# Two mixer attentions put into a written order, slot by slot, with the products of the branches between them

## The chip, the cores and the metric

One core of one Trainium2 chip. TensorE multiplies matrices, VectorE, ScalarE and GpSimd work on tiles, SyncE issues the DMAs; each takes its own instructions in order and waits on semaphores for the others. The metric is the device time of one execution in microseconds (us), as the median of several runs; lower is better.

## What is computed

Two blocks of a network run one after the other on one sequence of 512 positions with 1024 features. The first block has two layers of mixer, cross attention and FFN; only the mixer is touched. Cut to what matters here:

```python
def hybrid_mixer(x, ...):
    aq, ak, av, bq, bk, bv, cz, gate = split(x @ w_in)
    out_a = window_attention(rope(aq), rope(ak), av, sink)          # 8 heads of 64, 2 kv heads, band of 128
    out_b = dense_block_attention(rope(rms(bq)), rope(rms(bk)), bv)  # 8 heads of 64, all 512 keys
    out_c = spatial_gating(gelu(cz))
    gates = sigmoid(gate + b_gate)                                   # 3 branches x 1024
    merged = sum over n of (branch_n @ w_branch[n]) * gates[n]
    return merged @ w_mix_out
```

All products are done in a split form: each operand is rounded to a high part and a remainder, and high x high, high x low and low x high are added.

## The kernel before, in words

**Products.** `mm3` (L128) issues the three matmuls of one product, at L131, L132 and L133. A 128-row weight unit comes through `W` (L135): a 512 KB DMA on SyncE into one of two `wraw` tiles (L141), a rounding copy on ScalarE into one of three `wh` tiles (L146), a subtraction on VectorE into one of three `wl` tiles (L150).

**The mixer** (`mix`, L943) runs `gating` (branch c), then `heads_ab` for a (L726: projections by `tok`, rotary tables by `rope`, then `to_stack`, which transposes the queries on TensorE and splits them into tiles at L621 to L626, and `to_twice`, the same for the keys, L635 to L642), then `attn_a` (L783), `branch` for c (L920), `heads_ab` for b, `attn_b` (L829), `branch` for a and `branch` for b. Branch n makes 8 units: a gate product of 8 x 3 matmuls of 512 columns, a tanh (L930), an output product of 4 x 3 matmuls, and a merge (L938, or L940 and L941).

**One head** of attention: four score tiles (`mm2`, L649 and L650, into one of two `pss` banks), per tile a maximum on VectorE (L805 and L807 in a; L844, and in b L845 for the queries' norm, which is applied at the exponential) and an exponential with a row sum on ScalarE (L809, L847), a reciprocal and four scalings on VectorE (L818, L852), then `pt_av` (L693): transposes on TensorE (L703, two `pt` banks), a rounding copy on ScalarE (L166), a subtraction on VectorE (L167), and two matmuls (L713, L714) into the one `po` bank; `join` (L716) moves and adds the halves (L719, L720).

**What sets the order.** The program is traced in the order above, and the tile framework's planner then orders every engine's instructions when it builds the program (L1832, `schedule_with_timeline_sim=True`): at each moment of its own modelled time it takes, for an engine, the ready instruction that was traced first, and gives tiles their buffers as they come free. Only where a block stands in `behind(mark)` is an instruction held behind the marked one on the same engine. In the attentions and branches of before nothing is held: their interleaving is the planner's.

Of the kernel before, what the change touches and what calls it, by code (L numbers as in the profile page):

```python
# [7 lines left out]
F32R = mybir.dt.float32r  # L8
# [9 lines left out]
NK = 8  # L18
# [31 lines left out]
class Kernel:  # L50
# [76 lines left out]


# [6 lines left out]
    def W(self, ap, kc, tag=None):  # L135

# [8 lines left out]
        for i in range(n):  # L145
            nc.scalar.copy(h[i][:, :e], raw[:, i * e:(i + 1) * e])  # L146
        self.turn += 1
# [9 lines left out]
        return at  # L157
# [535 lines left out]
    def pt_av(self, out, pap, nkt, qr, vap, first=True, last=True, keep=None):  # L693


        nc = self.nc
        for kt in range(nkt):
# [11 lines left out]
            v, o = vap(kt), out[:, q0 * 128:q1 * 128]  # L709
            if isinstance(v, tuple):  # L710
                self.mm3(o, *v, h[:, :n], l[:, :n], first and kt == 0, last and kt == nkt - 1)
                continue
            nc.tensor.matmul(o, v, h[:, :n], start=first and kt == 0, stop=False, skip_group_check=True)  # L713
            nc.tensor.matmul(o, v, l[:, :n], start=False, stop=last and kt == nkt - 1, skip_group_check=True)  # L714

    def join(self, out, o, half):  # L716

        r, q = (slice(64 * i, 64 * i + 64) for i in (half, 1 - half))
        self.nc.scalar.copy(out[r], o[q])  # L719
        self.nc.vector.tensor_add(out[r], out[r], o[r])  # L720
# [5 lines left out]
    def heads_ab(self, l, br, xs, tabs, mid=None):  # L726
# [40 lines left out]
        rs = None  # L767
        if isb:
# [9 lines left out]
            rs = rq  # L778
        Q = [self.to_stack("q", [qt[c // 2, t // 2][:, t % 2, (c % 2) * 128:(c % 2 + 1) * 128] for t in range(4)]) for c in range(4)]
        Kt = self.to_twice("r", [kt[t // 2][:, t % 2, :] for t in range(4)])  # L780
        return Q, Kt, V, rs

    def attn_a(self, qkv, sink):  # L783
        nc = self.nc
        Q, Kt, V, _ = qkv
        nsink = self.sm(8)
        nc.vector.tensor_scalar(nsink, sink, -1.0, None, op0=ALU.mult)
        out = []
        for c in range(4):
            both = self.T("w")  # L790
            for half in range(2):
                o = self.po()
                hd = c + 4 * half
                kh, kl = Kt[half]
                P = []
                mx, nm, sm = self.sm(4), self.sm(4), self.sm(4)
                for qt in range(4):
                    k0, k1 = max(0, qt - 1), min(4, qt + 2)
                    n = (k1 - k0) * 128
                    ps = self.pss()  # L800
                    self.mm2(ps[:, :n], Q[c][half][:, qt * 128:(qt + 1) * 128], kh[:, k0 * 128:k1 * 128],
                             kl[:, k0 * 128:k1 * 128])
                    pt = self.T("vw"[half])
                    m0 = (k0 - qt + 1) * 128
                    nc.vector.tensor_tensor_reduce(pt[:, :n], ps[:, :n], self.mask[:, m0:m0 + n], 1.0, -3e38,  # L805
                                                   op0=ALU.add, op1=ALU.max, accum_out=mx[:, qt:qt + 1])
                    nc.vector.tensor_scalar(nm[:, qt:qt + 1], mx[:, qt:qt + 1], -0.125, nsink[:, hd:hd + 1],  # L807
                                            op0=ALU.mult, op1=ALU.min)
                    nc.scalar.activation(pt[:, :n], pt[:, :n], AF.Exp, bias=nm[:, qt:qt + 1], scale=0.125,  # L809
                                         accum_out=sm[:, qt:qt + 1])  # L810
                    P.append(pt)
                es = self.sm(4)
                nc.scalar.activation(es, nm, AF.Exp, bias=sink[:, hd:hd + 1])
                nc.vector.tensor_add(sm, sm, es)
                nc.vector.reciprocal(sm, sm)
                for qt in range(4):
                    n = (min(4, qt + 2) - max(0, qt - 1)) * 128
                    nc.vector.tensor_scalar(P[qt][:, :n], P[qt][:, :n], sm[:, qt:qt + 1], None, op0=ALU.mult)  # L818

                def pap(qt, kt):  # L820
                    o0 = (kt - max(0, qt - 1)) * 128
                    return P[qt][:, o0:o0 + 128]
                vap = lambda kt: V[kt // 2][:, kt % 2, 128 * half:128 * half + 128]
                self.pt_av(o, pap, 4, lambda kt: (max(0, kt - 1), min(4, kt + 2)), vap)
                self.join(both, o, half)
            out.append(self.split("o", both))
        return out

    def attn_b(self, qkv):  # L829
        nc = self.nc  # L830
        Q, Kt, V, rq = qkv
        out = []
        for c in range(4):
            both = self.T("w")
            for half in range(2):
                o = self.po()
                kh, kl = Kt[half]
                P = []
                nm, sm = self.sm(4), self.sm(4)
                for qt in range(4):  # L840
                    ps = self.pss()
                    self.mm2(ps, Q[c][half][:, qt * 128:(qt + 1) * 128], kh, kl)
                    i = ((c // 2) * 2 + qt // 2) * 8 + (qt % 2) * 4 + (c % 2) * 2 + half
                    nc.vector.tensor_reduce(nm[:, qt:qt + 1], ps, axis=AX.X, op=ALU.max, negate=True)  # L844
                    nc.vector.tensor_tensor(nm[:, qt:qt + 1], nm[:, qt:qt + 1], rq[:, i:i + 1], op=ALU.mult)  # L845
# [992 lines left out]
```

## Time and profile before

| | before |
|---|---|
| median of 3 runs | 3546.34 us (3545.05 to 3547.64) |
| the profiled execution's own time | 3543.88 us |
| its span, first to last instruction | 3542.1 us |
| TensorE busy, matmuls | 3396.8 us (96%), 19136 |
| VectorE, ScalarE, GpSimd busy | 2168.1, 1538.4, 386.6 us |
| mean granted TensorE clock | 0.98 of 2.4 GHz |

Busy matmul time is modelled and overlapping, so a busy share says that TensorE had something, not that it ran at its full pace; the number of matmuls per microsecond and the granted clock say that.

### The profile page before, as it was taken

The numbers are of one execution on the slowest core, as the hardware profiler recorded it, in microseconds if no ns is written. First come the engines' busy times: TensorE is split into PE (matmuls) and PEld (weight loads), VectorE is DVE, ScalarE is ACT, GpSimd is POOL, SyncE is SP. The second block draws the span as 40 slices with busy tenths as digits, with TensorE's granted clock in tenths as the row PEclk, the third lists the DMA queues.
The fourth block names the chain that finished last, engine by engine and source line by source line (L and its number), as shares of the span: only waits on it lengthen the run. The fifth ranks groups of instructions, "written<-read, shape, count | busy, mean of one in ns | idle before, by whom it ended". The sixth has DMA issues, their size and how long they took to land.

```text
span 3542.1 us, 49037 instructions
## 1 busy us (share of the span) xinstructions
PE 3396.8 (96%) x19136; PEld 2953.1 (83%) x19136; DVE 2168.1 (61%) x3926; ACT 1538.4 (43%) x2854; POOL 386.6 (11%) x588
## 2 busy tenths in 40 slices
PE   9989799999999897999999898999999998999999
PEld 8877598888898775998888897889888887988887
DVE  5675577645666755776456688655333698664333
ACT  3454445433444444455334556443222576442222
POOL 0000012000010000020000343000000286110000
PEclk9999899999999997999999998999999999999999
DMA  4312132333323120322333122222333322222333
GB/s 142 89 46 76 30 115 77 90 96 95 107 81 87 46 78 24 112 91 84 100 96 101 58 79 88 82 84 84 95 99 94 100 72 90 78 66 90 101 95 95
DMA packets 87928, 302.38 MB, mean 85 GB/s; under 512 B 10000, under 2 KB 10768, under 8 KB 87696
## 3 DMA queue, kind: packets, MB, share of 16 engines
q1 hardware_dynamic: 87696, 299.24, 28.0%
q8 instruction: 151, 2.47, 0.3%
q14 instruction: 81, 0.66, 0.1%
HBM read 297.10 MB, written 2.10 MB: 84 GB/s over the span
## 4 chain that ended last, share of the span: by engine, by line
PE 83%; DVE 7%; ACT 3%; POOL 3%; issue 2%; DMA 1%; ACTq 0%; POOLq 0%; DVEq 0%
PE mm L131 23%; PE mm L132 23%; PE mm L133 23%; PE pt L703 2%; PE mm L195 1%; PE pss L133 1%; PE pss L132 1%; PE pss L131 1%; DVE wl L150 1%; PE pss L649 1%; PE pss L650 1%; PE mm L198 1%; PE po L195 1%; PE po L714 1%; POOL v L1454 1%
## 5 line engine op out<-in xcount | busy, mean ns | idle before, releaser
L146 ACT CAST wh<-wraw 128x1024 fp32r<-128x1024 f32 (+2 forms) x496 | 514.3, 1040 | 959.8 <-PE mm L132 491.7
L150 DVE TENSOR_TENSOR wl<-wraw,wh 128x1024 fp32r<-128x1024 f32 (+2 forms) x487 | 599.5, 1233 | 501.6 <-ACT wh L146 499.0
L131 PE MATMUL mm<-xh,wh 128*128 128x512 f32 (+1 forms) x2152 | 821.8, 382 | 8.3 <-ACT xh L437 6.0
L132 PE MATMUL mm<-xl,wh 128*128 128x512 f32 (+1 forms) x2152 | 821.5, 382 | 1.2 <-DVE xl L440 1.1
L133 PE MATMUL mm<-xh,wl 128*128 128x512 f32 (+1 forms) x2152 | 819.7, 381 | 0.0
L131 PEld LDWEIGHTS mm<-xh,wh 128*128 128x128 f32 x2152 | 405.9, 189 | 83.6 <-ACT xh L437 6.4
L132 PEld LDWEIGHTS mm<-xl,wh 128*128 128x128 f32 x2152 | 406.1, 189 | 77.4 <-DVE xl L440 3.3
L133 PEld LDWEIGHTS mm<-xh,wl 128*128 128x128 f32 x2152 | 405.9, 189 | 75.8
L131 PE MATMUL mm<-wh,xh 128*128 128x256 f32 x768 | 219.7, 287 | 8.3 <-DVE v L671 8.3
L133 PE MATMUL mm<-wh,xl 128*128 128x256 f32 x768 | 219.6, 286 | 0.0
L132 PE MATMUL mm<-wl,xh 128*128 128x256 f32 x768 | 219.2, 286 | 0.0
L131 PE MATMUL mm<-p,wh 128*128 128x512 f32 (+1 forms) x556 | 202.1, 373 | 12.4 <-ACT p L166 7.7
L133 PE MATMUL mm<-p,wl 128*128 128x512 f32 (+1 forms) x556 | 206.4, 372 | 0.0
L132 PE MATMUL mm<-p,wh 128*128 128x512 f32 (+1 forms) x556 | 205.8, 371 | 0.0
L376 POOL TENSOR_TENSOR s<-s 128x2 f32<-128x2 f32 x14 | 6.8, 483 | 1617.4 <-ACT s L373 1617.4
L131 PE MATMUL mm<-o,wh 128*128 128x512 f32 (+1 forms) x456 | 169.3, 371 | 0.0
L132 PE MATMUL mm<-o,wh 128*128 128x512 f32 (+1 forms) x456 | 169.1, 371 | 0.0
L133 PE MATMUL mm<-o,wl 128*128 128x512 f32 (+1 forms) x456 | 169.1, 371 | 0.0
L1170 DVE TENSOR_TENSOR x<-x,mm 128x512 f32<-128x512 f32 (+1 forms) x102 | 57.0, 566 | 164.4 <-PE mm L133 164.3
L131 PEld LDWEIGHTS mm<-wh,xh 128*128 128x128 f32 x768 | 148.5, 194 | 9.4 <-issue 8.3
L132 PEld LDWEIGHTS mm<-wl,xh 128*128 128x128 f32 x768 | 148.7, 194 | 0.4
L133 PEld LDWEIGHTS mm<-wh,xl 128*128 128x128 f32 x768 | 148.7, 194 | 0.2
(628 smaller groups left out, 7133.3 us busy)
## 6 DMA issues: line engine op xcount, KB each, us to landing
wraw<-fup SPq DMA_DIRECT2D x88, 512.0 KB, 3.6
wraw<-gup SPq DMA_DIRECT2D x88, 512.0 KB, 3.6
wraw<-wg SPq DMA_DIRECT2D x48, 512.0 KB, 3.6
wraw<-wt SPq DMA_DIRECT2D x32, 512.0 KB, 3.6
wraw<-fdn SPq DMA_DIRECT2D x32, 512.0 KB, 3.5
wraw<-gdn SPq DMA_DIRECT2D x32, 512.0 KB, 3.5
wraw<-wbr SPq DMA_DIRECT2D x24, 512.0 KB, 3.6
wraw<-wab SPq DMA_DIRECT2D x20, 512.0 KB, 3.6
```

Source lines behind the costliest of these rows:

```text
L131: mm(out, lh, rh, start=first, stop=False, skip_group_check=True)
L132: mm(out, lh, rl, start=False, stop=False, skip_group_check=True)
L133: mm(out, ll, rh, start=False, stop=last, skip_group_check=True)
L146: nc.scalar.copy(h[i][:, :e], raw[:, i * e:(i + 1) * e])
L150: eng.tensor_tensor(l[i][:, :e], raw[:, i * e:(i + 1) * e], h[i][:, :e], op=ALU.subtract)
L195: self.nc.tensor.matmul(out, w[:, c], xs[k][0][:, t], start=first and k == 0 and w is h, stop=False, skip_group_check=True)
L198: self.nc.tensor.matmul(out, h[:, c], xs[k][1][:, t], start=False, stop=k == kc - 1, skip_group_check=True)
L649: mm(out, q, kh, start=True, stop=False, skip_group_check=True)
L650: mm(out, q, kl, start=False, stop=True, skip_group_check=True)
L703: nc.tensor.transpose(ps[:, i * 128:(i + 1) * 128], pap(qt, kt), self.ident)
L714: nc.tensor.matmul(o, v, l[:, :n], start=False, stop=last and kt == nkt - 1, skip_group_check=True)
L1170: self.nc.vector.tensor_add(x, x, ps)
```

## The change

`attn_a` and `attn_b` become one `attn`, which, like `branch`, no longer issues its work as it goes but lists events (slot, function). `weave` sorts the events of one attention and of the branches given to it by slot, and issues each behind the last one issued on every engine but SyncE, so that inside a weave the order on TensorE, VectorE, ScalarE and GpSimd is that of the slots. A head starts every 12 slots, and so does a branch unit. Attention a is woven with branch c, attention b with branches a and b. `W` is split in three steps (copy, subtraction, use), so that they have slots of their own. The first half of a head's scalings goes from VectorE to GpSimd. In b the norm is multiplied into the queries before the transposes (four 128x512 operations in `heads_ab`), and L845 goes.

```diff
+    def put(self, f):
+        n = len(self.nc.cur_bb.bb.instructions)
+        with self.behind(*self.seq.values()):
+            f()
+        for i in self.nc.cur_bb.bb.instructions[n:]:
+            if i.engine != self.nc.sync.engine:
+                self.seq[i.engine] = i
+
+    def weave(self, events):
+        self.seq = {}
+        for _, f in sorted(events, key=lambda e: e[0]):
+            self.put(f)
...
+            for i, (u, p) in enumerate((u, p) for u in range(2) for p in range(2)):
+                qv = qt[u, p].rearrange("p t (h c) -> p t h c", h=4)
+                r = rq[:, 8 * i:8 * i + 8].rearrange("p (t h) -> p t h", t=2)
+                nc.vector.tensor_tensor(qv, qv, r[:, :, :, None].to_broadcast([128, 2, 4, 64]), op=ALU.mult)
...
+            def norm(a):
+                e = slice(2 * a, 2 * a + 2)
+                if isa:
+                    nc.vector.tensor_add(st["sm"][:, e], st["sm"][:, e], st["es"][:, e])
+                nc.vector.reciprocal(st["sm"][:, e], st["sm"][:, e])
+                eng = nc.vector if a else nc.gpsimd
+                for qt in (2 * a, 2 * a + 1):
+                    p = P[qt][:, :width(qt)]
+                    eng.tensor_scalar(p, p, st["sm"][:, qt:qt + 1], None, op0=ALU.mult)
...
+            for j in range(4):
+                at(s0 + 3 * j, lambda j=j: score(j))
+                at(s0 + 3 * j + 1, lambda j=j: top(j))
+                at(s0 + 3 * j + 2, lambda j=j: exp(j))
+                at(s0 + 3 * j + 15, lambda j=j: turn(j))
+                at(s0 + 3 * j + 16, lambda j=j: high(j))
+                at(s0 + 3 * j + 17, lambda j=j: low(j))
+                at(s0 + 3 * j + 19, lambda j=j: weigh(j))
+            for a in range(2):
+                if isa:
+                    at(s0 + 6 * a + 5.5, lambda a=a: sinks(a))
+                at(s0 + 6 * a + 6, lambda a=a: norm(a))
+            at(s0 + 29, move)
+            at(s0 + 30, join)
+            if half:
+                at(s0 + 31, split_h)
+                at(s0 + 32, split_l)
+        for i in range(8):
+            head(i)
+        for slot, f in fill:
+            at(slot + 0.6, f)
+        self.weave(ev)
...
-    def branch(self, l, n, o, xs, mrg):
+    def branch(self, l, n, o, xs, mrg, s=0, lag=0, add_to=True):
...
+        for gate_ in (0, 1):
+            unit_at(gate_, 0, s - 2, s - 1)
         for k in range(NK):
+            so, sg = (s + 12 * k, s + 12 * k + 4) if k >= lag else (s + 8 * lag + 4 * k, s + 8 * k)
+            if k + 1 < NK:
+                unit_at(1, k + 1, *((so + 1, so + 3) if k >= lag else (sg + 1, sg + 3)))
+                if k % 2 and k >= lag:
+                    unit_at(0, k // 2 + 1, so + 6, so + 9)
...
+            for q in range(4):
+                at(so + q, lambda k=k, q=q: out(k, q))
             for q in range(NK):
+                at(sg + q, lambda k=k, q=q: gate(k, q))
+            at(sg + 8, lambda k=k: tanh(k))
+            e = max(so + 4, sg + 8)
+            at(e + 1, lambda k=k: merge(k))
+            if add_to:
+                at(e + 2, lambda k=k: add(k))
...
-        self.branch(l, 2, oc, xs, mrg)
+        self.attn("a", qkv, sink, oa, self.branch(l, 2, oc, xs, mrg, add_to=False))
...
-        ob = self.attn_b(qkv)
-        self.branch(l, 0, oa, xs, mrg)
-        self.branch(l, 1, ob, xs, mrg)
+        self.attn("b", qkv, None, ob, self.branch(l, 0, oa, xs, mrg) + self.branch(l, 1, ob, xs, mrg, 96, 3))
```

`head(i)` sets `s0 = 12 * i`. `score` is the two matmuls of a tile, `top` the maximum, `exp` the exponential, `turn` the transposes, `high` and `low` the copy and the subtraction after them, `weigh` the two matmuls into `po`, `move` and `join` the former `join`; in `branch`, `out` and `gate` are one `mm3` each, and `unit_at` sets the copy (with the DMA) and the subtraction of a weight unit. The numbers of matmuls, transposes and weight loads are those of before.

## Rows read from the trace of the kernel before

**Rows 1.** The chain that ended last, by engine, share of the span

```profile
PE 83%; DVE 7%; ACT 3%; POOL 3%; issue 2%; DMA 1%; ACTq 0%; POOLq 0%; DVEq 0%
```

**Rows 2.** Windows, first mixer: stretch, busy us and (instructions) per engine, clock, DMA, GB/s

```profile
96.00:190.00 94.00, 94.00 (x518) 81.95 (x517) 56.61 (x127) 46.04 (x89) 0.00 (x0) 1.00 0.27 81
190.00:246.00 56.00, 46.41 (x292) 40.03 (x291) 44.97 (x143) 27.41 (x71) 0.00 (x0) 0.91 0.13 38
246.00:330.00 84.00, 84.00 (x400) 69.91 (x398) 56.44 (x105) 39.53 (x65) 0.00 (x0) 1.00 0.27 83
330.00:423.00 93.00, 71.09 (x281) 47.19 (x279) 55.69 (x116) 44.10 (x87) 0.00 (x0) 0.89 0.06 17
```

**Rows 3.** Windows of the FFN and of `tok`, and transposes in the timeline

```profile
2500.00:2550.00 50.00, 50.00 (x222) 41.40 (x221) 19.20 (x22) 11.77 (x13) 0.00 (x0) 1.00 0.32 95
...
80.00:90.00 10.00, 10.00 (x85) 10.00 (x85) 8.97 (x15) 2.71 (x4) 0.00 (x0) 1.00 0.38 116
...
194.20 0.38 PE L703 MATMUL pt<-ident,w 128*128 128x128 f32 x2
...
194.54 0.49 PE L703 MATMUL pt<-ident,w 128*128 128x128 f32 x3
```

**Rows 4.** Matmuls by tile: ns min/median/max, first and last start us; both mixers

```profile
L131 PE MATMUL mm<-wh,xh x87: 283/283/333, 59.8 to 96.1; 128*128 128x256 f32 x87
...
L649 PE MATMUL pss<-r,q x6: 277/306/339, 121.0 to 133.1; 128*128 128x256 f32 x3, 128*128 128x384 f32 x3
...
L131 PE MATMUL mm<-wh,xh x48: 277/283/415, 220.3 to 245.5; 128*128 128x256 f32 x48
...
L649 PE MATMUL pss<-r,q x6: 389/389/389, 272.9 to 290.8; 128*128 128x512 f32 x6
...
L131 PE MATMUL mm<-p,wh x20: 389/389/389, 428.6 to 463.2; 128*128 128x512 f32 x20
...
L131 PE MATMUL mm<-wh,xh x123: 283/283/333, 1019.9 to 1070.5; 128*128 128x256 f32 x123
...
L131 PE MATMUL mm<-p,wh x20: 389/389/389, 1407.4 to 1442.1; 128*128 128x512 f32 x20
```

**Rows 5.** Groups by form, 96 to 464 us: busy us, mean ns, idle before

```profile
L150 DVE TENSOR_TENSOR wl<-wraw,wh 128x1024 fp32r<-128x1024 f32 x42 | 51.4, 1223 | 44.6 <-ACT wh L146 44.1
L167 DVE TENSOR_TENSOR t<-pt,t 128x512 fp32r<-128x512 f32 x32 | 21.7, 688 | 21.4 <-ACT t L166 21.3
L844 DVE TENSOR_REDUCE s<-pss 128x1 f32<-128x512 f32 x32 | 21.6, 688 | 9.2 <-PE pss L650 9.1
L941 DVE TENSOR_TENSOR m<-m,f 128x512 f32<-128x512 f32 x15 | 10.3, 689 | 0.3
L852 DVE TENSOR_SCALAR w<-w,s 128x512 f32<-128x512 f32 x16 | 6.7, 482 | 0.1
...
L146 ACT CAST wh<-wraw 128x1024 fp32r<-128x1024 f32 x42 | 44.2, 1052 | 60.7 <-PE mm L132 45.7 <-PE mm L133 7.7 <-issue 7.4
...
L847 ACT ACTIVATE w<-pss,s 128x512 f32<-128x512 f32 x16 | 12.3, 774 | 7.6 <-DVE s L845 7.5
L625 ACT CAST q<-pt 64x512 fp32r<-64x512 f32 x16 | 9.3, 582 | 10.5 <-DVE q L626 5.7 <-PE pt L621 4.7
```

**Rows 6.** Timeline of VectorE at the end of `heads_ab` for b

```profile
256.15 0.20 DVE L301 SCALAR_TENSOR_TENSOR s<-s 128x40 f32<-128x40 f32 x1
...
256.86 0.20 DVE L301 SCALAR_TENSOR_TENSOR s<-s 128x40 f32<-128x40 f32 x1
257.10 0.76 DVE L775 TENSOR_TENSOR w<-w,s 128x256 f32<-128x256 f32 x2
```

**Rows 7.** GpSimd: a group by form, then GpSimd and VectorE in the timeline

```profile
L991 POOL TENSOR_TENSOR p<-w,p 128x512 fp32r<-128x512 f32 x4 | 5.6, 1414 | 0.0
...
511.24 0.74 POOL L413 TENSOR_TENSOR x<-x,c 128x256 f32<-128x256 f32 x1 [4.70 <-DVE x L408]
...
511.34 1.72 DVE L150 TENSOR_TENSOR wl<-wraw,wh 128x1024 fp32r<-128x1024 f32 x1
```

More of the change, by code (lines that the diff above doesn't have):

```diff
@@ L135, in W, with W_steps @@
     def W(self, ap, kc, tag=None):
+        steps = self.W_steps(ap, kc, tag)
+        next(steps)
+        next(steps)
+        return next(steps)
+    def W_steps(self, ap, kc, tag=None):
         nc = self.nc
@@ L146, in W @@
             nc.scalar.copy(h[i][:, :e], raw[:, i * e:(i + 1) * e])
+        yield
         self.turn += 1
@@ L156, in at @@
             return h[k // kp][:, s], l[k // kp][:, s]
-        return at
+        yield
+        yield at
     def split(self, role, src, n=512, scale=None):
@@ L708, in pt_av @@
                 h, l = keep[kt]
[L709 to L720, printed above, removed]
+            vh, vl = vap(kt)
+            self.mm3(out[:, q0 * 128:q1 * 128], vh, vl, h[:, :n], l[:, :n], first and kt == 0, last and kt == nkt - 1)
     def wt(self, l, g):
@@ L780, in heads_ab, with attn @@
         Kt = self.to_twice("r", [kt[t // 2][:, t % 2, :] for t in range(4)])
-        return Q, Kt, V, rs
-    def attn_a(self, qkv, sink):
+        return Q, Kt, V
+    def attn(self, br, qkv, sink, out, fill):
         nc = self.nc
[L785 to L845, printed above, removed]
-                    pt = self.T("vw"[half])
-                    nc.scalar.activation(pt, ps, AF.Exp, bias=nm[:, qt:qt + 1], scale=rq[:, i:i + 1],
-                                         accum_out=sm[:, qt:qt + 1])
-                    P.append(pt)
-                nc.vector.reciprocal(sm, sm)
-                for qt in range(4):
-                    nc.vector.tensor_scalar(P[qt], P[qt], sm[:, qt:qt + 1], None, op0=ALU.mult)
-                vap = lambda kt: V[kt // 2][:, kt % 2, 128 * half:128 * half + 128]
-                self.pt_av(o, lambda qt, kt: P[qt][:, kt * 128:(kt + 1) * 128], 4, lambda kt: (0, 4), vap)
-                self.join(both, o, half)
-            out.append(self.split("p", both))
-        return out
@@ L859, in gating @@
+        both = []
+        for i in range(8):
[3 more added lines that the diff above has]
+        self.weave(ev)
     def gating(self, l, xs, cb, bs, oc):
@@ L955, in mix @@
         qkv = self.heads_ab(l, "a", xs, ta, lambda: next(g))
-        oa = self.attn_a(qkv, sink)
-        mrg = {}
-        self.branch(l, 2, oc, xs, mrg)
+        oa, ob, mrg = [], [], {}
+        self.attn("a", qkv, sink, oa, self.branch(l, 2, oc, xs, mrg, add_to=False))
         tb, tq = self.T("c"), [self.T("c"), self.T("c")]
```

129 lines of the change are left out of this document (109 added, 20 removed).

## The prediction, made before the run

> **What bounds the kernel now.** I read the chain of waits first: 83% of it is TensorE [rows 1], so a change pays only where TensorE has something to win back. Then the windows, to find where that is. In the FFN TensorE issues 222 matmuls of 512 columns in 50 us, 0.225 us each; the projections by `tok` (256 columns) take 10 us for 85, 0.118 each; a transpose adds 0.11 (0.38 for two, 0.49 for three) [rows 3]. I call that the dense pace; for 384 columns I take 0.172, halfway.
>
> In the mixer two stretches are dense and two are not [rows 2]. From 96 to 190 us and from 246 to 330 TensorE is busy throughout at clock 1.00: there the planner has woven heads with branch c, and later with branch a. From 190 to 246 and from 330 to 423 it is busy 46.4 of 56 us and 71.1 of 93, at clocks 0.91 and 0.89: the branch that could fill has been used up, or (branch b) needs attention b's output, and the remaining heads run almost alone. VectorE is at 60 to 80% and ScalarE at 47 to 49% in all four, so neither is the bound; it is latency, head after head.
>
> The loss in numbers. The stretch runs from the last `tok` of a's heads (its last high product starts at 96.1) to the last output product of branch b (463.2, with its triple 463.9) [rows 4]: 367.5 us. Its TensorE work at the dense pace:
> - 24 branch units x 36 x 0.225 = 194.4;
> - 8 heads of b: 8 score matmuls 1.8, 8 in `po` 1.8, 16 transposes 1.76; 5.4 each, 42.9;
> - 8 heads of a: 2 x (4 x 0.118 + 4 x 0.172) + 10 x 0.11 = 3.4 each, 27.4;
> - `tok` for b, 288 x 0.118 = 34.0; 40 transposes of queries and keys, 4.4.
>
> Together 303; lost 64. The second mixer runs from 1070.5 to 1442.1 and its triple, 372.3 [rows 4], with the same work: lost 69. **133 us in all is what the change can reach.**
>
> **The change, part by part.**
>
> *The weave itself.* TensorE's work is the same. A period of 12 slots holds one head's attention work and one branch unit: 8.1 + 3.4 = 11.5 us in a, 8.1 + 5.4 = 13.5 in b. VectorE per period in b: 4 maxima and 4 `low` at 0.69, `join`, merge and add at 0.69, half a split 0.34, two scalings 0.96, one and a half weight subtractions 1.83, reciprocals 0.4 by the small operations of [rows 6]: 11.1 us of 13.5 [rows 5]. In a, with tiles 320 columns wide on average and no add, about 9.5 of 11.5. ScalarE: 4 x 0.77, 4 copies and a move at 0.58, a tanh 0.77, half a split 0.3, 1.05 + 0.53 of weight copies: 8.7 [rows 5]. So TensorE is the longest in each period. Does strict order stall it? I placed b's period by hand: the tightest place is the single `po` bank. `weigh` 3 of a head starts 5.0 us into a period; `move` and `join` follow; the next head's first `weigh` is due at 8.35; with VectorE's queue in order, `join` ends near 7.5. Slack 0.9 us. Every other wait (two `pss`, two `pt`, three `mm` banks, three `wh`) has over 1.5 us. So the stall per head lies between 0 (the dense windows of rows 2) and a slipped slot, about 1.1 us; I take 0.5 for 16 heads, **8 us a mixer**.
>
> *Weight loads.* 24 gate and output units as before. The DMAs stay outside the chain, so SyncE issues them when a `wraw` tile is free; a unit comes 12 slots after the one whose tile it takes. Price 0; the cover is those 11 us, and without it a load shows whole.
>
> *The norm put ahead in b.* Off: 32 small operations of about 0.2 us on VectorE. On: four of 512 columns, 0.69 each by L941 [rows 5]. The former were covered; the latter stand before the first score (next).
>
> *The new wait: the start of each weave.* TensorE's chain starts with `score` 0, which needs queries and keys, and every branch product is queued behind it. In before, the gates ran meanwhile: between the last `tok` product and the first score lie 24.9 us in a and 27.4 in b [rows 4], all dense. Now nothing covers this.
> - a: four query stacks, whose copies and subtractions take turns on one bank (copies wait for the subtraction, 5.7 us in all [rows 5]): transposes 0.44, first copy 0.58, 8 x 0.69, 0.35 of waiting per stack; 7.9. Then the keys' transposes 0.44 and two pairs of 0.58 + 0.69; 10.9 us. TensorE does 20 transposes in it, 2.2: lost **8.7**.
> - b: squares, sums and rotation of the keys, six operations at 0.38; three Newton rounds at 0.71; key scaling 0.76 [rows 6]; two small ones 0.4; 5.6. Four query scalings 2.8, one query subtraction 0.69, then the keys' subtraction, copy and subtraction 2.0: 11.1, lost **8.9**.
>
> Bounds: these, where the planner lets the shortest way go first, and before's own 24.9 and 27.4, where it does not. I take the lower, because in before VectorE and ScalarE had weights and merges to serve between these steps, and in the weave those are held behind them.
>
> *The clock.* Between 330 and 423 TensorE idled 21.9 us and the granted clock was 0.89, which is 20 of the 93 us at the lower level, 1.2 GHz [rows 2]. Two idle stretches of 9 us would bring some 8 us each at that level; from none to all of it can fall on matmuls afterwards, 0 to 4 us lost. I take 2.5 each, **5**.
>
> *The end of a's weave.* Branch c ends at slot 96, the last head at 116. `tok` for b (34 us) is not held and can fill; its rotations need tiles that the last head frees. **3 us**. *The end of b's*: branch b's gates 0 to 2 stand in slots 96 to 120 beside the last head; the last unit now ends with its gate and a tanh of 0.77: **1**.
>
> *Half the scalings on GpSimd.* Nine slots of room for two operations of at most 1.41 us each by a 512-column row [rows 7]: 0 directly; what it does to VectorE is a rival below.
>
> **Sum.** Left per mixer: 8.7 + 8.9 + 5 + 3 + 8 + 1 = 35, so 70 of 133 stays and 63 goes. The profiled execution took 3543.9 us (span 3542.1); the median, 3546.3, is 2.5 above it. I set the sum against the median: 3546 - 63 = **3483 us**.
>
> **Rivals.**
> 1. *VectorE blocked by GpSimd.* A weight subtraction, both inputs in SBUF, took 1.72 us instead of 1.22 beside a GpSimd operation of 0.74 [rows 5, 7]. If VectorE stands still for two GpSimd scalings a head (2.8 us in b, 2.1 in a), its period is 13.9 and 11.6: it becomes the bound by 0.4 and 0.1, and with lateness handed on I allow 0.5 a head: 16 us over both mixers, 3499. The Trainium skill, "SBUF — State Buffer", section "Who interferes with whom", has it as an exclusive lock: whichever of GpSimd and a VectorE instruction with two SBUF inputs comes second blocks fully. By that rule the trace agrees: 0.5 us is about what was left of the 0.74.
> 2. *The starts are as long as before's.* Lost 22.7 and 25.2 instead of 8.7 and 8.9, 30 more a mixer: 3543. For: the planner takes what was traced first, queries before keys. Against: little else is then ready.
> 3. *Shorter*: no stall per head, no clock, a's end covered. 16 less a mixer: 3451.
> 4. *Slower: the single `po` bank.* If VectorE reaches `join` late by more than the 0.9 us, TensorE waits in each head, with all branch products behind it, where the planner of before would have run one. Late by one weight subtraction, a merge, an add and a `low` (3.3 us), the price is 2.4 us x 32 heads = 77: 3560. It decides from 2.0 us a head on, where the gain is gone. Against: VectorE has 2.4 us free per period in b.
> 5. *It does not do what it says*: the planner's own weave is dense where material lasts; the losses reappear where the written order runs out. 3546.
>
> **How the numbers follow.** Chances: forecast 0.58, rival 1 0.12, rival 2 0.08 (half of it reaching only 3530 or so), rival 3 0.10, rival 4 0.07, rival 5 0.05. Range: rival 3's 3451 less a little, 3448, up to 3530, the half way to rival 2; outside are rivals 4 and 5 and half of 2, 0.16, and some of 3. Measurement can tell 0.2%, 7 us. Faster 0.58 + 0.12 + 0.10 + 0.04 = 0.84; same 0.05 + 0.04 = 0.09; slower 0.07.
>
> **What the profile would show.** Right: both non-dense stretches gone, TensorE at clock 1.00 from the first score to the end of each weave, and two idle stretches of 9 us a mixer before the first scores, put down in the waits to the split of the keys or queries. Rival 1: weight subtractions well over 1.22 us in the mixers and TensorE waiting for `low`. Rival 2: idle stretches near 25 us. Rival 4: the first `po` matmul waiting for the add of `join`, once per head. Wrong altogether: waits of a microsecond spread over all slots.

## The result, and the profile after

| | before | after |
|---|---|---|
| median | 3545.93 us (3545.05 to 3547.64, 4 runs) | 3484.92 us (3484.20 to 3486.43, 4 runs) |
| ratio after to before | | 0.9828, 95% interval 0.9811 to 0.9845 |
| span of the profiled execution | 3542.1 us | 3483.0 us |
| mean granted TensorE clock | 0.980 | 0.982 |

The forecast was 3483; the measured gain is 61 us of the 63 that I had worked out. The sum came out; two of its terms (the start of b's weave, and the stalls inside the weaves) did not, and they nearly cancelled.

First the page of the changed kernel: busy time per engine, the granted clock in 40 slices, and the chain that ended last (answers to [rows 1]).

```profile
PE 3355.8 (96%) x19136; PEld 2939.5 (84%) x19136; DVE 2153.8 (62%) x3854; ACT 1537.5 (44%) x2870; POOL 473.1 (14%) x652
...
PEclk9989999999999899999999999999999999999999
...
PE 84%; DVE 8%; ACT 3%; POOL 2%; issue 2%; DMA 1%; ACTq 0%; POOLq 0%; DVEq 0%
```

The number of matmuls is unchanged, and the shares of the chain are those of [rows 1] within a point: nothing was removed from TensorE, only its idle time. (GpSimd's 473.1 us were 386.6.) So the next view is where, as in [rows 2]: windows of the first mixer, with the bounds set at the new stages (length, then busy us and instructions of PE, PEld, DVE, ACT, POOL, clock, DMA share, GB/s).

```profile
96.00:108.00 12.00, 4.33 (x22) 2.85 (x20) 8.54 (x15) 7.13 (x13) 0.00 (x0) 0.72 0.00 0
108.00:238.00 130.00, 130.00 (x783) 115.86 (x783) 95.01 (x256) 69.61 (x158) 18.45 (x16) 0.99 0.25 75
238.00:258.00 20.00, 7.16 (x26) 4.88 (x25) 14.46 (x37) 8.07 (x14) 0.00 (x0) 0.58 0.00 1
258.00:385.00 127.00, 126.78 (x612) 104.28 (x611) 86.23 (x141) 69.01 (x133) 25.48 (x16) 0.99 0.20 59
385.00:433.00 48.00, 48.00 (x214) 39.74 (x213) 21.84 (x26) 14.85 (x19) 0.00 (x0) 1.00 0.34 100
```

The two thin stretches of [rows 2] are gone: from 108 to 238 and from 258 on TensorE is busy throughout at clock 0.99. In their place stand two short idle stretches, 96 to 108 and 238 to 258, the starts of the two weaves, with clocks of 0.72 and 0.58 and no DMA traffic. Their edges are to be had from the matmuls by line (ns min/median/max, first and last start us), as in [rows 4]:

```profile
L146 PE MATMUL mm<-wh,xh x85: 283/283/332, 59.9 to 95.5; 128*128 128x256 f32 x85
...
L673 PE MATMUL pss<-r,q x46: 277/422/797, 107.2 to 298.9; 128*128 128x256 f32 x16, 128*128 128x384 f32 x16, 128*128 128x512 f32 x14
...
L146 PE MATMUL mm<-wh,xh x89: 278/283/364, 201.4 to 237.7; 128*128 128x256 f32 x89
...
L673 PE MATMUL pss<-r,q x14: 389/475/797, 256.3 to 298.9; 128*128 128x512 f32 x14
...
L146 PE MATMUL mm<-wh,xh x101: 283/283/333, 1000.0 to 1042.7; 128*128 128x256 f32 x101
```

Last `tok` product of a to first score: 95.5 to 107.2, 11.7 us. Of b: 237.7 to 256.3, 18.6 us. The last `tok` of a in the second mixer starts at 1042.7 where it was 1070.5 [rows 4], and the first mixer's is 0.6 earlier than before: the first mixer saved 27.2 us of the 59.1 by which the span shrank, the second, with what follows it, 31.3.

To compare kernels I count much as in the prediction: each matmul that starts in a window of 10 us is set at the dense pace (here 0.227 us for 512 columns, 0.174 for 384, 0.118 for 256, 0.109 for a transpose; the prediction had 0.225, 0.172, 0.118 and 0.11), and what is left of the window is lost. Summed over stretches of the first mixer, in us:

| kernel (time) | 90-130, a's start | 130-220, a's weave | 220-270, b's start | 270-400, b's weave | 400-480 | sum |
|---|---|---|---|---|---|---|
| before (3545.9) | 0.0 | 14.5 | 6.3 | 27.0 | 15.0 | 62.8 |
| after (3484.9) | 11.8 | 1.0 | 19.1 | 1.9 | 3.1 | 36.9 |
| e1_free (3446.8) | 0.1 | 3.7 | 0.3 | 7.2 | 4.4 | 15.7 |
| e2_dve (3482.8) | 13.0 | 1.1 | 18.0 | 1.8 | 2.6 | 36.5 |
| e3_keys_first (3456.4) | 5.7 | 1.1 | 11.3 | 1.7 | 2.9 | 22.7 |
| e4_cover (3476.9) | 5.0 | 6.1 | 12.9 | 6.2 | 3.1 | 33.3 |
| e5_join_plus4 (3505.4) | 12.0 | 5.3 | 18.7 | 7.4 | 2.2 | 45.6 |
| e5_join_plus8 (3578.1) | 12.6 | 19.1 | 13.3 | 30.1 | 5.8 | 80.9 |
| e7_free_keys (3437.4) | 0.3 | 1.0 | 1.9 | 6.6 | 3.8 | 13.6 |
| e8_hold_pe (3484.8) | 13.2 | 1.4 | 19.7 | 1.5 | 3.0 | 38.8 |
| e9_keys_gate (3451.6) | 2.6 | 1.7 | 7.1 | 6.7 | 3.5 | 21.6 |
| e10_free_start (3452.3) | 6.6 | 1.1 | 7.6 | 1.7 | 3.3 | 20.3 |
| e11_scale_late (3475.0) | 11.4 | 1.1 | 14.8 | 2.0 | 3.8 | 33.1 |
| e12_free_keys_late (3443.3) | 0.2 | 1.3 | 2.0 | 10.2 | 3.6 | 17.3 |

Twice the difference of two sums (two mixers) is close to the difference of the times: after to e3_keys_first 28.4 against 28.5, to e5_join_plus8 88 against 93, and within some 5 us for the other kernels. From before to after it is 52 against 61, since the table has the first mixer only and its last column takes in the next stage's beginning in after but not in before. Counted instead in each mixer from the last `tok` of a's heads to the last product of branch b, the loss is 62.6 and 66.8 us before and 33.7 and 35.1 after: 60.6 us less, where the span shrank by 59.1. So the count can be read as the account of the change. Nearly all that is left of its loss, 30.9 of 36.9, lies in the two starts; inside the weaves 1.0 and 1.9 are left. (Where a kernel is much later than the others, as e5_join_plus8, its stages are shifted against the columns.)

What TensorE waits for in the second start, after (us in total, times, longest):

```profile
PE pt L645 <- DVE w L793: 6.3, 1, 6.3
PE pt L645 <- DVE q L650: 3.4, 2, 2.4
PE pss L673 <- ACT r L665: 2.2, 1, 2.2
PE pt L659 <- DVE q L650: 1.0, 1, 1.0
```

And VectorE's timeline there (start us, us; L787 scales the keys, L793 the queries, L650 splits a query stack, L666 the keys):

```profile
242.92 0.76 DVE L787 TENSOR_TENSOR w<-w,s 128x256 f32<-128x256 f32 x2
...
243.81 2.50 DVE L793 TENSOR_TENSOR w<-w,s 128x512 f32<-128x512 f32 x4
246.75 0.68 DVE L650 TENSOR_TENSOR q<-pt,q 64x512 fp32r<-64x512 f32 x1 [0.44 <-ACT q L649]
248.08 1.41 DVE L650 TENSOR_TENSOR q<-pt,q 64x512 fp32r<-64x512 f32 x2 [0.65 <-ACT q L649]
250.13 1.41 DVE L650 TENSOR_TENSOR q<-pt,q 64x512 fp32r<-64x512 f32 x2 [0.65 <-ACT q L649]
252.19 1.41 DVE L650 TENSOR_TENSOR q<-pt,q 64x512 fp32r<-64x512 f32 x2 [0.65 <-ACT q L649]
254.24 0.69 DVE L650 TENSOR_TENSOR q<-pt,q 64x512 fp32r<-64x512 f32 x1 [0.65 <-ACT q L649]
254.97 0.68 DVE L666 TENSOR_TENSOR r<-pt,r 64x512 fp32r<-64x512 f32 x1
```

The keys are scaled at 242.9, but their split comes after four query scalings (2.50) and after all four query stacks, one every 2.05 us from 246.1 to 254.2: the first head needs one of these stacks. Copies on ScalarE and subtractions on VectorE take turns (0.65 idle in each), as they did before [rows 5].

In before, where the stacks are made of unscaled queries, four of the eight query subtractions (there L626) also came after the keys' scaling at 257.10 [rows 6]:

```profile
258.70 0.68 DVE L626 TENSOR_TENSOR q<-pt,q 64x512 fp32r<-64x512 f32 x1
...
264.12 0.69 DVE L626 TENSOR_TENSOR q<-pt,q 64x512 fp32r<-64x512 f32 x1
```

### The profile page after: what moved, and what is told of

It reads as the page before. It is cut to its first block, busy times and chain, and to the rows that moved or that the text cites. A ratio compares the mean times of both kernels' runs of the same rounds, so it can differ in the third digit from the quotient of the medians.

```text
span 3483.0 us, 49091 instructions
## 1 busy us (share of the span) xinstructions
PE 3355.8 (96%) x19136; PEld 2939.5 (84%) x19136; DVE 2153.8 (62%) x3854; ACT 1537.5 (44%) x2870; POOL 473.1 (14%) x652
## 4 chain that ended last, share of the span: by engine, by line
PE 84%; DVE 8%; ACT 3%; POOL 2%; issue 2%; DMA 1%; ACTq 0%; POOLq 0%; DVEq 0%
PE mm L146 24%; PE mm L147 23%; PE mm L148 23%; PE mm L219 1%; PE po L879 1%; PE pt L863 1%; DVE wl L173 1%; PE pss L674 1%; DVE pss L1563 1%; PE pss L673 1%; PE pss L148 1%; PE pss L147 1%; PE po L219 1%; PE pss L146 1%; PE mm L222 1%
## 5 line engine op out<-in xcount | busy, mean ns | idle before, releaser
L312 POOL TENSOR_TENSOR s<-s,mhalf 128x2 f32<-128x2 f32 (+1 forms) x45 | 39.2, 872 | 853.2 <-ACT s L473 568.3
```

The lines of the kernel that those rows point to most:

```text
L312: e.tensor_tensor(y, v, self.mhalf.to_broadcast([128, n]), op=ALU.pow)
```

## The experiments

Each kernel is the changed one with the edit shown, unless said; ratios are to the kernel before. They were run in four sets, each beside its own runs of before (medians 3545.8 to 3548.6 us), so a few microseconds between kernels of different sets say little by themselves.

### Is it the hold, and whose

**e1_free.** The events are issued in the order of their slots, but nothing is held: the planner may take them as it likes, and prefers what stands earlier.

```diff
-        with self.behind(*self.seq.values()):
-            f()
+        f()
```

> The events are traced in the order of their slots, as in the change, but none is held behind another, so the planner may depart from that order. Theory A, what pays is that branch material is spread over all heads, and the slot order of the trace is enough for that: the planner then also runs gate products while it waits for the first score (about 10 to 18 us of the four starts each come back, some of it lost again where the material runs out later): 3440 to 3480 us. Theory B, the gain hangs on the held order, and the planner without it falls back to runs of heads without material: 3520 to 3546 us.

Measured: 3446.78 us (3446.13 to 3448.28), 0.9716 (0.9701 to 0.9730): theory A. Its windows:

```profile
90.00:130.00 40.00, 40.00 (x213) 34.34 (x212) 23.97 (x43) 19.79 (x31) 0.00 (x0) 1.00 0.30 88
...
220.00:270.00 50.00, 50.00 (x265) 42.85 (x265) 37.98 (x76) 21.72 (x35) 0.53 (x1) 1.00 0.32 95
...
350.00:370.00 20.00, 16.11 (x80) 11.31 (x78) 15.71 (x28) 12.53 (x27) 3.86 (x3) 1.00 0.00 0
```

Both starts are dense at clock 1.00: gates run there. The price is inside the weaves (3.7 and 7.2 us in the table instead of 1.0 and 1.9), above all at 350 to 370, where the last heads have no branch material left (DMA 0.00). So the change is two things of opposite sign: writing the program in the order of the slots, with the change's smaller parts (GpSimd's half, the scaled queries, the split `W`), is worth 99 us, and holding it to that order takes 38 of them back. Of the smaller parts, e2_dve and e11_scale_late below undo two in the held program; no run has the order of the slots without any of them.

**e8_hold_pe.** Only TensorE's instructions are marks of the order.

```diff
-            if i.engine != self.nc.sync.engine:
+            if i.engine == self.nc.tensor.engine:
                 self.seq[i.engine] = i
```

> Only TensorE's instructions of the slots are held in order; an instruction of another engine is merely not put ahead of TensorE's last one before it. Theory A (what costs the changed kernel its 35 us against the program without holds is TensorE's order alone, with gates queued behind the first score): no difference from the changed kernel, 3478 to 3488. Theory B (the orders of VectorE and ScalarE cost by themselves, by keeping the splits of queries and keys of the start, or the copies of weights, behind others): some 10 us or more below it, 3446 to 3474. Theory C (the other engines' order is what keeps the weave dense): slower, over 3490.

Measured: 3484.83 us (3483.44 to 3489.14), 0.9830 (0.9815 to 0.9845), starts of 13.2 and 19.7: theory A. The order of the other engines neither costs nor gains anything here that can be measured; TensorE's alone keeps the gates out of the starts.

### GpSimd's half of the scalings

**e2_dve.** All scalings of `norm` on VectorE.

```diff
-                eng = nc.vector if a else nc.gpsimd
+                eng = nc.vector
```

> All four scalings of a head on VectorE again, none on GpSimd. Theory A, GpSimd's half neither blocks VectorE nor relieves the bound, since VectorE has over 2 us free in each period: within 5 us of the changed kernel, 3480 to 3490 us. Theory B (GpSimd's scalings block weight subtractions): 5 to 16 us faster, 3469 to 3480 us. Theory C (VectorE is so close to the bound that 1 us more in each of 32 periods shows): 10 to 30 us slower, 3495 to 3515 us.

Measured: 3482.82 us (3480.55 to 3485.86), 0.9817 (0.9803 to 0.9832), which can't be told from the change's 0.9828 (0.9811 to 0.9845). Theory A; rival 1 falls, and so does VectorE as a bound. In the changed kernel, weight subtractions over both weaves, and one beside GpSimd:

```profile
L173 DVE TENSOR_TENSOR wl<-wraw,wh x41: 1209/1220/1227, 109.7 to 427.5; 128x1024 fp32r<-128x1024 f32 x41
...
274.81 3.11 POOL L856 TENSOR_SCALAR w<-w,s 128x512 f32<-128x512 f32 x2 [7.49 <-DVE s L852]
...
276.89 1.22 DVE L173 TENSOR_TENSOR wl<-wraw,wh 128x1024 fp32r<-128x1024 f32 x1
```

None of the 41 is longer than 1.227 us, though six of them began while the profile has a scaling on GpSimd. Where rival 1 asked for subtractions well over 1.22, there is none.

### The single `po` bank

In the changed kernel the hand-over looks like this (the last product of a head, `move`, `join`, the next head's first product):

```profile
286.46 0.63 PE L879 MATMUL po<-t,r 128*128 128x512 f32 x2
...
287.12 0.59 ACT L886 COPY w<-po 64x512 f32<-64x512 f32 x1 [0.98 <-PE po L879]
...
287.74 0.68 DVE L889 TENSOR_TENSOR w<-w,po 64x512 f32<-64x512 f32 x1 [0.38 <-ACT w L886]
...
289.89 0.63 PE L879 MATMUL po<-t,r 128*128 128x512 f32 x2
```

`join` ends at 288.42 and the next `weigh` starts at 289.89: slack 1.46 us, where I had placed 0.9. **e5_join_plus4** uses it up with four passes of VectorE, **e5_join_plus8** with eight (`range(8)`):

```diff
             def join():
+                for _ in range(4):
+                    nc.vector.tensor_scalar(both[c][r], both[c][r], 1.0, None, op0=ALU.mult)
```

> The changed kernel, with four more VectorE passes (a product with 1.0 over the 64 x 512 that the add of join is to change) ahead of that add in every head; the values stay. This tests the slack of the one po bank, which my rival 4 put at 0.9 us. In the changed kernel the add ends 1.46 us (head at 287.7, branch b of the attention) and 1.26 us (head at 146.9, a) before the next head's first po product starts, and a scaling of 512 columns on VectorE took 0.45 us, so four passes add 1.8. Theory A (that slack is all there is, and what is late by more is handed on to TensorE whole): 0.35 to 0.55 us in each of 28 hand-overs, 10 to 15 us: 3494 to 3500. Theory B (the order held in the slots has more give than one hand-over shows, for VectorE idles some 2 us a period): within 4 us of the changed kernel, 3481 to 3489.

> The same with eight passes, 3.6 us a head. Theory A: 2.1 to 2.35 us late in each of 28 hand-overs, 59 to 66 us: 3543 to 3551, and each pass beyond the slack costs 28 x 0.45 = 13 us. Theory C (it is not the hand-over but VectorE's whole period that decides: 11.1 + 3.6 = 14.7 against 13.5 us in b, 9.5 + 3.6 = 13.1 against 11.5 in a): 1.2 x 16 + 1.6 x 16 = 45 us, 3530, and then four passes cost nothing. Theory B: under 3500.

Measured: 3505.35 us (3501.34 to 3507.07), 0.9882 (0.9865 to 0.9898), with four; 3578.11 us (3572.05 to 3581.01), 1.0089 (1.0074 to 1.0104), with eight. Theories B and C fall. Theory A has the wait right, but the times grew by more than it gave: by 20 and 93 us, where it had 10 to 15 and 59 to 66. The hand-over with eight passes:

```profile
309.69 3.59 DVE L890 TENSOR_SCALAR w<-w 64x512 f32<-64x512 f32 x8 [0.38 <-ACT w L886]
...
313.38 0.68 DVE L891 TENSOR_TENSOR w<-w,po 64x512 f32<-64x512 f32 x1
...
314.21 1.19 PE L879 MATMUL po<-t,r 128*128 128x512 f32 x2 [2.22 <-DVE s L852]
```

and the weave's window of it:

```profile
258.00:385.00 127.00, 100.40 (x447) 80.04 (x448) 96.97 (x187) 57.75 (x113) 21.52 (x14) 0.87 0.14 42
```

The wait is the one named (its releaser is put down to the reciprocal that stands right behind the add, 0.2 us before), 2.22 us long as theory A has it. TensorE's waits for `po` over both mixers, 90 to 1425 us (L851 and L852 are that reciprocal's):

```profile
PE po L879 <- DVE w L891: 30.2, 12, 3.5
...
PE po L879 <- DVE s L851: 14.5, 6, 2.4
PE po L879 <- DVE s L852: 13.3, 6, 2.2
```

That is 58.0 us in 24 hand-overs (14.2 with four passes, none in the changed kernel), close to theory A's amounts. What A left out is seen beside it: the pair of products after the wait at 314.21 takes 1.19 us instead of 0.63, and the clock of the weave is 0.87 instead of 0.99, so part of the 127 us ran at 1.2 GHz. Over both mixers the trace has 126 us at that level, and 68 in the changed kernel; 58 us more at half the pace are up to 29 us lost (an estimate from these two), which with the 58.0 of waits makes 87 of the 93. The remaining 6 stay open, as do some 4 of the 20 with four passes (72 us at the lower level). Rival 4's mechanism is thus real; it did not decide because VectorE reaches `join` 1.46 us ahead. VectorE's idle time in other places does not help.

### The length of the starts

**e3_keys_first.** The keys are turned and split ahead of the query stacks, in a and in b.

```diff
-        Q = [self.to_stack("q", [...]) for c in range(4)]
         Kt = self.to_twice("r", [kt[t // 2][:, t % 2, :] for t in range(4)])
+        Q = [self.to_stack("q", [...]) for c in range(4)]
```

> The keys are transposed and split ahead of the four query stacks, nothing else. Theory A, what is left of the loss is the wait of TensorE's chain for score 0, and score 0 needs the keys and one query stack only: each of the four starts is shorter by three stacks of 2.05 us, 6 us, and a little of the clock comes back: 3455 to 3463 us. Theory B, the starts are set by what VectorE and ScalarE have to do altogether before a head can run densely: the first score comes earlier and the next ones wait for the stacks, 3475 to 3485 us.

Measured: 3456.39 us (3455.12 to 3458.33), 0.9744 (0.9728 to 0.9760): theory A. The first scores now start at 101.0 and 241.9, the last `tok` products before them at 95.9 and 231.8 (rows of this kernel, as above):

```profile
L673 PE MATMUL pss<-r,q x9: 277/363/522, 101.0 to 124.2; 128*128 128x256 f32 x5, 128*128 128x384 f32 x4
...
L673 PE MATMUL pss<-r,q x18: 389/475/764, 241.9 to 298.7; 128*128 128x512 f32 x18
```

5.1 and 10.1 us instead of 11.7 and 18.6: three query stacks now lie beside the first head instead of ahead of it.

**e11_scale_late.** The queries' scaling of b undone; the factor goes back to the maxima and the exponentials.

```diff
-                nc.vector.tensor_tensor(qv, qv, r[:, :, :, None].to_broadcast([128, 2, 4, 64]), op=ALU.mult)
...
+                    nc.vector.tensor_tensor(st["nm"][:, e], st["nm"][:, e], rqc(qt), op=ALU.mult)
...
-                                     scale=0.125 if isa else 1.0, accum_out=st["sm"][:, e])
+                                     scale=0.125 if isa else rqc(qt), accum_out=st["sm"][:, e])
```

> The changed kernel with one part of the change undone: the queries of b are not scaled ahead of their stacks; the factor is applied to each maximum and in each exponential, as before. Theory A (my working for b's start took the query stacks to be built before the scaling, as they were before; in the changed kernel all four must wait for it, 2.05 us each from 246.1 to 254.2 us, so the scaling costs not its own 2.5 us but 8 to 10): the stacks go back beside the projections, the first score of b follows the last projection product by 9 to 11 us instead of 19.5, and the time is 3484.9 - 2 x (8 to 10) = 3465 to 3469; the 32 small operations are covered. Theory B (the stacks stay behind the projections' own work, and only the four scalings go): 17 us from the last projection product to the first score, 3478 to 3481.

Measured: 3475.02 us (3473.16 to 3475.93), 0.9798 (0.9785 to 0.9812): between the two. The last `tok` product starts at 236.8, the first score at 250.8, 14.0 us. VectorE's timeline:

```profile
239.63 0.68 DVE L650 TENSOR_TENSOR q<-pt,q 64x512 fp32r<-64x512 f32 x1
...
245.75 0.76 DVE L787 TENSOR_TENSOR w<-w,s 128x256 f32<-128x256 f32 x2
...
246.64 1.41 DVE L650 TENSOR_TENSOR q<-pt,q 64x512 fp32r<-64x512 f32 x2
248.69 0.69 DVE L650 TENSOR_TENSOR q<-pt,q 64x512 fp32r<-64x512 f32 x1 [0.65 <-ACT q L649]
```

Freed of the scaling, five of the eight query subtractions slip between the small operations of the norm, from 239.6 on; three still come after the keys' scaling at 245.75, which is itself 2.8 us later. So the scaling costs b's start 4.6 us (18.6 less 14.0): its own 2.5 and part of the stacks behind it, less than A's 8 to 10 because the stacks fall among the key norm's work.

### Covering the starts

**e4_cover.** The queries first, as in the change, but branches moved ahead: c by three gates, a by two, b to slot 90.

```diff
-        self.attn("a", ..., self.branch(l, 2, oc, xs, mrg, add_to=False))
+        self.attn("a", ..., self.branch(l, 2, oc, xs, mrg, -24, 3, False))
-        self.attn("b", ..., self.branch(l, 0, oa, xs, mrg) + self.branch(l, 1, ob, xs, mrg, 96, 3))
+        self.attn("b", ..., self.branch(l, 0, oa, xs, mrg, -16, 2) + self.branch(l, 1, ob, xs, mrg, 90, 3))
```

> The branches begin before the heads: branch c with three gates ahead (slots -24 to 0), branch a with two (-16 to 0), branch b at 90 in place of 96, so that TensorE's chain begins with 16.2 and 10.8 us of gate products. Theory A, the starts (11.6 us lost in a, 19 in b, by the trace) cost because nothing stands ahead of score 0: a's goes to about 1, b's to about 8, and 10 slots without material before branch b cost 3 to 5 a mixer: 2 x (10.6 + 11 - 4) = 35 faster, 3445 to 3455 us. Theory B, gates ahead put weight copies and subtractions on ScalarE and VectorE into the way from the last projection to score 0, and lengthen it towards the 25 and 27 us of before: 3465 to 3485 us.

Measured: 3476.94 us (3476.75 to 3478.58), 0.9801 (0.9787 to 0.9816): B's number, and B's way too. From the last `tok` product to the first score it is now 21.5 us in a and 23.2 in b, where the change has 11.7 and 18.6, so the 16.2 and 10.8 us of gates take only 6.8 and 6.2 off the losses of the starts (11.8 to 5.0, 19.1 to 12.9). And the weaves lost 6.1 and 6.2 where they had lost 1.0 and 1.9, which neither theory has in this size:

```profile
210.00:220.00 10.00, 7.46 (x43) 6.55 (x42) 8.82 (x30) 5.11 (x15) 2.15 (x2) 0.83 0.01 0
...
350.00:360.00 10.00, 6.84 (x31) 4.03 (x30) 9.36 (x16) 6.73 (x14) 0.30 (x2) 1.00 0.11 24
```

**e9_keys_gate.** Keys first as in e3_keys_first, and one gate ahead in either weave.

```diff
-        self.attn("a", ..., self.branch(l, 2, oc, xs, mrg, add_to=False))
+        self.attn("a", ..., self.branch(l, 2, oc, xs, mrg, -8, 1, False))
-        self.attn("b", ..., self.branch(l, 0, oa, xs, mrg) + self.branch(l, 1, ob, xs, mrg, 96, 3))
+        self.attn("b", ..., self.branch(l, 0, oa, xs, mrg, -8, 1) + self.branch(l, 1, ob, xs, mrg, 92, 3))
```

> The changed kernel, held in its slots, with the keys first and the branches moved ahead by one gate: branch c and branch a begin at slot -8 with one gate before their outputs, branch b at 92 instead of 96. Theory A (holding costs nothing by itself; what it costs is only that nothing written stands in the start): the keys-first kernel lost 5.5 us at a's start and 10.8 at b's; a gate is 24 products, 5.4 us; the starts shrink to 0 to 1 and 5 to 6, 3456.4 - 2 x 10 = 3434 to 3442, which is where the program without holds and with the keys first stands (3437.4). Theory B (material moved to the start is missing at the end, as in the kernel with three and two gates ahead, where new holes of 5.0 and 4.8 us opened): 3446 to 3456.

Measured: 3451.60 us (3450.26 to 3454.54), 0.9737 (0.9724 to 0.9750): B's number again. The losses of the starts shrank to 2.6 and 7.1 (from the last `tok` to the first score 8.8 and 11.2 us, without the gate 5.1 and 10.1), and a hole opened at 340 to 350:

```profile
340.00:350.00 10.00, 6.84 (x25) 4.64 (x24) 8.02 (x12) 7.19 (x14) 4.83 (x2) 0.83 0.34 105
```

Branch a now ends at slot 88, and the first gate of branch b stands at 92, with the copies and subtractions of its first two weight units at 90 and 91. From 341.6 ScalarE makes two weight copies in a row, and VectorE two weight subtractions after them; TensorE waits 1.1 us for a copy, 1.2 for a subtraction and 0.9 for `join`. By the trace, then, it is the four slots that I left empty between the branches, with the weights prepared too late to fill them. No run has those slots filled, and that the material as a whole was short, as B says, this kernel does not show.

**e10_free_start.** Keys first, and the slots held only from slot 24 on.

```diff
-        for _, f in sorted(events, key=lambda e: e[0]):
-            self.put(f)
+        for slot, f in sorted(events, key=lambda e: e[0]):
+            f() if slot < 24 else self.put(f)
```

> The keys first, and the slots held only from slot 24 on: what stands in the first two heads' slots (two gates and their outputs among it) is the planner's to order. Theory A (the 16.3 us a mixer that the keys-first kernel loses are only a matter of what may run in the starts): the two units, 16 us of TensorE, cover both, and 3437 to 3445 results. Theory B (what covers the start is missing in the first two heads, which then run almost alone, as heads did before the change): 3450 to 3458, no gain of over 6 us on 3456.4.

Measured: 3452.26 us (3450.79 to 3453.97), 0.9735 (0.9722 to 0.9749): theory B. The two units run in the wait, and the first heads then go almost alone:

```profile
230.00:250.00 20.00, 20.00 (x103) 17.02 (x102) 17.37 (x44) 7.69 (x13) 0.00 (x0) 1.00 0.38 106
...
250.00:270.00 20.00, 15.33 (x73) 10.30 (x72) 18.87 (x33) 14.98 (x33) 6.44 (x4) 1.00 0.00 0
```

### Together

**e7_free_keys**: the edits of e1_free and e3_keys_first.

```diff
-        with self.behind(*self.seq.values()):
-            f()
+        f()
...
-        Q = [self.to_stack("q", [...]) for c in range(4)]
         Kt = self.to_twice("r", [kt[t // 2][:, t % 2, :] for t in range(4)])
+        Q = [self.to_stack("q", [...]) for c in range(4)]
```

> Both edits that helped, together: the program in the order of the slots, but none of them held (3446.8 alone), and the keys turned before the queries (3456.4 alone). Theory A (the planner without holds covers the starts with gates, and pays for it later, where the material runs out: 3.1 us lost at 200 to 210 and 6.5 at 350 to 370 in the first mixer; shorter starts use less of it): 5 to 10 us below 3446.8, 3436 to 3442. Theory B (the two edits win back the same microseconds, since a covered start costs nothing however long): 3445 to 3449.

Measured: 3437.40 us (3436.97 to 3438.01), 0.9694 (0.9680 to 0.9709): theory A, and the best of all these kernels, 47.5 us under the change. The starts are covered and short (12.0 and 21.3 us from the last `tok` to the first score, where e1_free has 27.4 and 35.9), so material lasts longer:

```profile
220.00:270.00 50.00, 48.73 (x249) 40.67 (x248) 39.90 (x79) 25.73 (x46) 6.64 (x4) 1.00 0.28 82
270.00:350.00 80.00, 80.00 (x399) 66.24 (x398) 56.63 (x94) 46.41 (x92) 18.56 (x11) 1.00 0.20 56
350.00:370.00 20.00, 17.18 (x78) 13.01 (x78) 12.79 (x22) 9.70 (x18) 1.76 (x2) 0.91 0.06 24
```

**e12_free_keys_late**: these two and the edit of e11_scale_late, of which its main line is

```diff
-                                     scale=0.125 if isa else 1.0, accum_out=st["sm"][:, e])
+                                     scale=0.125 if isa else rqc(qt), accum_out=st["sm"][:, e])
```

> Three edits together: no holds, keys first, queries of b scaled late. Theory A (a start that is shorter uses less material even where the planner covers it, and the hole of 5.8 us at 350 to 370 in the keys-first program without holds shrinks): 4 to 10 us below 3437.4, 3427 to 3433. Theory B (that hole is the last head of b by itself, which has no material in any order, and the 32 small operations lengthen each head's way from score to exponential): 3436 to 3446.

Measured: 3443.34 us (3440.81 to 3443.74), 0.9707 (0.9694 to 0.9720): B's number. The hole of b's weave grew (10.2 instead of 6.6), and b's start is hardly shorter (21.0 us from the last `tok` to the first score instead of 21.3), so theory A's premise did not come about. Whether the 32 small operations cause the hole, or only the other order that the planner finds, stays open; and as the ratios' intervals overlap, it is the lack of a gain that is shown, not a loss. So what e11_scale_late gains where the start is bare, it does not where the start is covered.

## Why the prediction was right

**The whole.** Left of the loss per mixer: forecast 35; measured 33.7 and 35.1 over the stretches that the forecast meant. The table's 36.9 for the first mixer has 3.1 past 400 us, in the next stage's beginning, which the sum had not counted. By its own steps, with the table's columns:

- *What bounds it, and what can be reached*: held. The thin stretches went, and matmuls and busy shares stayed.
- *The start of a*, 8.7 and 2.5 for the clock, 11.2: measured 11.8. The working (four stacks at some 2 us, then the keys) is what the trace shows: queries are split from 97.62 to 105.80 us, the keys from 105.84 on, and the first score starts at 107.2.
- *The start of b*, 8.9 and 2.5, 11.4: measured 19.1. **This step failed**: "one query subtraction 0.69, then the keys' subtraction". It took seven of the eight query subtractions to be done by then, since stacks of before are made of unscaled queries and need not wait for the norm. That was too much even for before, where four of the eight come after the keys' scaling (the rows of before above). After the change each reads a scaled query, so all four stacks stand behind the key norm and ahead of the keys: some 8 us for the term of 0.69. e11_scale_late shows that part of it is the scaling, e3_keys_first that 8.5 of the 18.6 us are the order of keys and queries.
- *The stall per head*, 0.5 us, 8 a mixer, the *end of a's weave*, 3, and the *end of b's*, 1: 12 together, measured 1.0 + 1.9. My bounds, 0 and a slipped slot, were right, and I chose too far from the lower one. The `po` slack that made me choose is 1.46 us, not 0.9, and TensorE does not wait there at all.
- *The clock*, 2.5 a start: borne out, as far as it can be told apart. In 238 to 258 the clock was granted at 0.58, with score matmuls of 797 ns instead of 389. The trace has it at 0.54 from 107 to 112 us and 0.52 from 256 to 262, when TensorE was busy again, and at 1.00 right after: an estimate of 2 to 3 us lost in each, inside the measured 11.8 and 19.1.
- *Scalings on GpSimd at 0*: held (e2_dve), though one of 512 columns took 1.57 us instead of the 1.41 assumed.

So 7.7 too little in b's start and 9 too much inside the weaves nearly cancelled. What bounds the kernel and where the loss goes was understood; that the sum came as near as 2 us was luck.

**The rivals.** 1 (GpSimd blocks VectorE): excluded by e2_dve. 2 (starts as long as before's): a's, no; b's 18.6 us is about half the way to it (from the 11.1 worked out to before's 27.4), and the reason I gave for it (what was traced first is taken first, queries before keys) is what happened; the reason against it (little else is then ready) was wrong: the scaled queries became ready only after the keys (243.81 against 242.92), and were taken first all the same. Why the planner let the keys wait for them stays open. 3 (no stall, a's end covered): right about the weaves. 4 (`po`): the mechanism exists, 1.46 us of slack kept it away, and eight passes of VectorE turn the change into a loss. 5: excluded by the windows. That the order, without the hold, would gain 38 us more stood in none of them: I had priced the cover lost at the starts, but not asked for the kernel that keeps it.

## What to carry to other kernels

Writing a program in the interleaved order and holding the engines to that order are two changes, and here the first (with the change's smaller parts) brought 99 us and the second cost 38: try the order without the hold first. Where an order is held, the stretch before its first instruction is bare; walk the chain to that instruction, item by item in the order of the program, and put what the first instruction needs ahead of what later ones need. Work that is moved into a gap is missing elsewhere: a cover pays only where there is spare material, and the gates moved ahead here also lengthened the way that they were to cover (11.7 to 21.5 us). Putting the keys first paid in either case, 28 us where the start was bare and 9 where it was covered.

## What the runs showed of the hardware

*GpSimd and VectorE.* In the changed kernel it is GpSimd that waits, if either: its scalings of 384 columns took 1245 ns on one set of tiles and 1558 on the other, while VectorE's 41 weight subtractions lay within 1209 to 1227 ns.

```profile
L856 POOL TENSOR_SCALAR w<-w,s 128x384 f32<-128x384 f32 x4 | 6.2, 1558 | 0.0
L856 POOL TENSOR_SCALAR v<-v,s 128x384 f32<-128x384 f32 x4 | 5.0, 1245 | 0.0
```

Of the slower set, one took 1245 ns like the others, and the three longer ones (1490 to 1750) began within 0.3 us of a VectorE subtraction of 0.69 us with both inputs in SBUF (L896). In e9_keys_gate one pair of GpSimd's scalings, beside two weight subtractions in a row, took 4.83 us instead of 3.11, and L896 right after those two 1.09 instead of 0.69. The Trainium skill, "SBUF — State Buffer", section "Who interferes with whom", has whoever comes second block; these longer operations, and the 1.72 us of [rows 7], agree with it in kind. But six weight subtractions of the changed kernel began while a scaling was on GpSimd by the profile (that at 276.89, above, is one) and took 1.209 to 1.224 us, where by that rule each should have been held up. The spans of GpSimd are rough, and no run here settles it.

*The clock.* In the stretches around the two starts, 96 to 108 us and 238 to 258, TensorE was mostly idle and its granted clock was 0.72 and 0.58, so part of each was at 1.2 GHz; the first score matmuls after them took up to 797 ns, twice their 389. With eight passes before `join` TensorE waits 2.2 to 2.5 us at most hand-overs. After some of these waits the products ran at about half pace (the pair at 314.21 took 1.19 us instead of 0.63), after others nearly at full pace (the pair at 331.90 took 0.70): waits of that length, repeated, cost more than themselves.
